# A hand-laid order for the attention, and modulation rows made in the layer that uses them

## The chip, the core and the metric

The kernel runs on one core of one Trainium2 chip. The metric is the time of one execution in microseconds of the device (us); lower is better. The engines meant below are PE (matrix multiplication), DVE (vector work on rows and columns), ACT (functions of one input, such as exp, and copies), POOL (a slower vector engine) and SP, which issues the transfers from the chip's memory. Each engine takes its instructions in the order in which they stand in its own queue; a semaphore makes one wait for another.

## The reference, cut to what matters

Two layers work on 1024 rows of 1024 numbers, in float32. A layer is a token mixer (convolution group, differential attention, gated chunk group, one output projection) and a channel mixer (up-projection to 2 x 2816, convolution of width 3, silu gate, down-projection). Each mixer is wrapped by a modulation from the conditioning vector `c`, and by a layer norm.

```python
c_act = jax.nn.silu(c)
for l in range(DEPTH):                                   # DEPTH = 2
    mod = (c_act @ w_ada[l] + b_ada[l])[:, None, :]
    sh1, sc1, g1, sh2, sc2, g2 = jnp.split(mod, 6, axis=-1)
    h = x * (1.0 + sc1) + sh1
    ...
    y = jnp.concatenate([y_a, y_b, y_c], axis=-1) @ w_out[l] + b_out[l]
    x = layer_norm(DEEPNORM_ALPHA * x + (1.0 + g1) * y, ln_g[l, 0], ln_b[l, 0])
    h = x * (1.0 + sc2) + sh2
    y = conv_ffn(h, w_up[l], b_up[l], conv_f_w[l], conv_f_b[l], w_down[l], b_down[l])
    x = layer_norm(DEEPNORM_ALPHA * x + (1.0 + g2) * y, ln_g[l, 1], ln_b[l, 1])
```

The six pieces of `mod` are numbered 0 to 5 in the kernel. 0, 1 and 2 (shift, scale, gate) belong to the token mixer, 3, 4 and 5 to the channel mixer.

The attention has 4 heads. A head has two softmax maps, each with its own queries and keys of 64 numbers; the values are 128 wide.

```python
for i in range(seq // ATTN_BLOCK):                       # 8 blocks of 128 queries
    s = jnp.einsum("bhmqd,bhmkd->bhmqk", qb, kb) * scale # m = 2 maps, keys 0 .. end
    p = jax.nn.softmax(jnp.where(mask, s, -jnp.inf), axis=-1)
    a = p[:, :, 0] - lam * p[:, :, 1]
    outs.append(jnp.einsum("bhqk,bhke->bhqe", a, vb))
o = rms_norm(o, subln_g) * (1.0 - lam_init)
```

## The kernel before

**Number format.** Every large product is split into a high and a low part and made of three matmuls (hi*hi, lo*hi, hi*lo; lines 130 to 132). A float32 operand is split by one ACT cast (line 125, tiles ending in `h`) and one subtraction on POOL or DVE (line 126, tiles ending in `l` or `L`).

**Stages of a layer.** First the modulated rows `h` are projected (`prj`, `ptm`), the convolution group and the chunk group are computed, and the queries, keys and values are written to memory. Then comes the attention with the first part of the output projection beside it. The rest of that projection (`og`), the residual and the layer norm follow (`boundary`: the rows are transposed back to columns, `tr`, line 333). Then the up-projection (`upb`), the down-projection (`og<-dn`) and a second `boundary`.

**The attention.** There are 32 units in a layer: 4 heads by 8 query blocks, in the order 7, 6, 3, 5, 2, 4, 1, 0 of the block number `i` (7, 6, 5, 4, 0, 1, 2, 3 in the last head). A unit has (i+1)*128 keys. One unit is: score matmuls on PE for both maps (line 733) and a mask (735); row maxima on DVE (754 or 756); exp with row sums on ACT (759); `rc`, `rho` and the difference of the two maps on DVE (762 to 767, here called diff); transposes on PE (774), copied by ACT (775); the product with the values on PE (778); scaling and sum of squares on ACT (780, 781). A unit with i of 4 or more is large: its two maps need two PSUM tiles of 1024 columns, and there are two; a small unit holds both maps in one tile. After a head come its norm (POOL line 138, DVE 789) and 8 transposes (801).

**The fill.** PE work that does not hang on the softmax is laid between: 16 chunks of the output projection over the convolution and chunk groups (4 row groups of `w_out`, 12 matmuls a chunk; here fillA) and 16 chunks over heads 0 and 1 (6 matmuls a chunk; here fill0). Each chunk ends in one PSUM bank, the only one of its kind, and DVE adds it to a row tile `r` (line 862, fill-add). Their weights are loaded, multiplied by the gate on POOL (`wout`, line 682), cast on ACT (`woh`) and subtracted on POOL (`wol`). In layer 0, POOL also adds a row to each of eight `r` tiles (line 871).

**What sets the order.** The code names units, heads and fills in program order, and a scheduler then lays each engine's queue by its own estimates and priorities. So a fill chunk can start before all of its weights are there, parts of several units interleave, and a late operand is passed by other work.

**The modulations.** Piece `idx` of layer `l` is one row of 1024: eight loads of 512 KB of `w_ada`, each multiplied and added on DVE (`macc` or `wada`, lines 258 and 260), then 8 one-column matmuls (`modp`, line 269) and small DVE work; a gate piece (2, 5) also has a transpose (`gatet`, line 286). A generator yields them in steps, one DVE operation over 1024 numbers in most. Before the change, layer 0's pieces 2 and 4 are made in its first stage, 3 in its attention, 5 at the start of its up-projection; all six of layer 1 (1, 0, 2, 3, 4, 5) follow in layer 0's up-projection (one step a tile of it) and what is left there (`later`) in layer 0's down-projection.

## Time and profile before

| what | us |
|---|---|
| median of 3 runs | 2440.98 (2439.22 to 2441.18) |
| the profiled execution | 2437.79 |
| its span | 2436.1 |
| first stage, layer 0 / layer 1, from `ptm` on | 205.0 / 190.1 |
| attention, layer 0 / layer 1 | 221.0 / 216.1 |
| up-projection, layer 0 / layer 1 | 426.2 / 422.8 |
| down-projection, layer 0 / layer 1 | 249.2 / 241.0 |
| from the last `og` of layer 0 to the first `prj` of layer 1 | 41.4 |

The stages are cut by PE's own rows: the attention runs from the first score matmul to the first `og` that follows (286.1 to 507.1 and 1492.1 to 1708.2 us of the span). PE is busy for 95% of the span, so a time is mostly read from what PE does and from the places where it stands still. A row of a timeline or of a group list has the line, the engine, the operation, what is written and read, and behind it the idle time of the engine just before, with what ended it.

### The profile page before, as it was taken

To read this page: it belongs to the slowest core of one execution; us is meant where nothing else is said; L and a number is where in the kernel's file an instruction comes from. 1 tells how busy PE (TensorE), PEld (TensorE's weight loads), DVE (VectorE), ACT (ScalarE), POOL (GpSimd) and SP (SyncE) were. 2 spreads that over 40 slices of the span, in tenths; PEclk is the share of its full clock that TensorE was granted. 3 is DMA by queue.
4 is the path that set the end of the run, shared out by engine and by line. 5 is a ranking of instruction groups with operands and counts; after the bars stand their busy time and mean duration, and the time that the engine had idled before them with its cause. 6 is when DMAs were issued, how large, how long until landed. Compare 5 with 4: busy or idle time off the path is not lost.

```text
span 2436.1 us, 28260 instructions
## 1 busy us (share of the span) xinstructions
PE 2308.1 (95%) x10846; PEld 1886.4 (77%) x10846; DVE 1956.1 (80%) x2650; ACT 1049.9 (43%) x1692; POOL 328.9 (13%) x165
## 2 busy tenths in 40 slices
PE   8998999979999999999959999999899999999996
PEld 7787778767888887788848877777688888878885
DVE  7898876778887888877978988657987777797857
ACT  4214754646554555311130257555654555561111
POOL 1143260410000000000020541214100000000003
PEclk9998999999999999999979999999999999999998
DMA  7433462122332333745523244320232222254301
GB/s 294 156 116 120 140 224 104 61 95 90 110 113 88 112 113 121 263 141 179 190 70 117 78 143 160 130 95 27 99 100 87 78 78 87 87 176 169 122 26 69
DMA packets 87672, 294.06 MB, mean 121 GB/s; under 512 B 9265, under 2 KB 18801, under 8 KB 86001
## 3 DMA queue, kind: packets, MB, share of 16 engines
q1 hardware_dynamic: 87536, 292.26, 35.4%
q8 instruction: 85, 1.39, 0.2%
q14 instruction: 51, 0.41, 0.1%
HBM read 228.23 MB, written 64.00 MB: 120 GB/s over the span
## 4 chain that ended last, share of the span: by engine, by line
PE 67%; DVE 17%; issue 6%; ACT 4%; DMA 3%; POOL 2%; SPq 0%; POOLq 0%; DVEq 0%; ACTq 0%
PE upb L1083 6%; PE upb L1084 6%; PE upb L1085 6%; PE og L130 5%; PE og L131 5%; PE og L132 5%; PE sc L733 3%; PE upd L1084 3%; PE upd L1085 3%; PE upd L1083 3%; DVE convacc L410 2%; PE pv L778 2%; PE of L130 2%; PE of L132 2%; PE of L131 2%
## 5 line engine op out<-in xcount | busy, mean ns | idle before, releaser
L1083 PE MATMUL upb<-comb,uw 128*128 128x512 f32 x704 | 274.9, 391 | 9.9 <-DVE upc L1107 5.0
L130 PE MATMUL og<-dn,dn 128*128 128x512 f32 x704 | 275.3, 391 | 2.6 <-ACT r L885 2.1
L131 PE MATMUL og<-dn,dn 128*128 128x512 f32 x704 | 274.5, 390 | 0.0
L132 PE MATMUL og<-dn,dn 128*128 128x512 f32 x704 | 274.3, 390 | 0.0
L1084 PE MATMUL upb<-comb,uw 128*128 128x512 f32 x704 | 274.0, 389 | 0.0
L1085 PE MATMUL upb<-comb,uw 128*128 128x512 f32 x704 | 273.9, 389 | 0.0
L1107 DVE TENSOR_TENSOR uw<-wu,uw 128x512 fp32r<-128x512 f32 x210 | 144.1, 686 | 125.3 <-ACT uw L1110 125.3
L1120 DVE SCALAR_TENSOR_TENSOR cv<-upc,pc,cv 128x1023 f32<-128x1023 f32 (+1 forms) x176 | 225.4, 1280 | 2.9
L138 POOL TENSOR_TENSOR lnrs<-lnrs,mhalf 128x1 f32<-128x1 f32 x32 | 24.8, 779 | 1421.4 <-DVE lnrs L137 1414.9
L887 DVE TENSOR_TENSOR r<-og,r 128x1024 f32<-128x1024 f32 x128 | 155.7, 1218 | 59.0 <-PE og L132 58.4
L410 DVE SCALAR_TENSOR_TENSOR convacc<-convy,pc,convacc 128x1023 f32<-128x1023 f32 (+14 forms) x120 | 176.2, 1469 | 2.3
L125 ACT CAST dn<-actr 128x1024 fp32r<-128x1024 f32 x44 | 46.1, 1049 | 298.1 <-issue 224.4
L1083 PEld LDWEIGHTS upb<-comb,uw 128*128 128x128 f32 x704 | 132.1, 188 | 41.0 <-DVE upc L1107 6.7
L1110 ACT CAST uw<-wu 128x512 fp32r<-128x512 f32 x210 | 121.7, 616 | 83.6 <-DVE wu L1107 77.1
L130 PEld LDWEIGHTS og<-dn,dn 128*128 128x128 f32 x704 | 132.2, 188 | 31.5 <-ACT r L885 3.4
L1085 PEld LDWEIGHTS upb<-comb,uw 128*128 128x128 f32 x704 | 132.2, 188 | 27.5
L132 PEld LDWEIGHTS og<-dn,dn 128*128 128x128 f32 x704 | 132.2, 188 | 27.4
L1084 PEld LDWEIGHTS upb<-comb,uw 128*128 128x128 f32 x704 | 132.2, 188 | 27.2
L131 PEld LDWEIGHTS og<-dn,dn 128*128 128x128 f32 x704 | 132.2, 188 | 26.8
L1083 PE MATMUL upd<-comb,uw 128*128 128x512 f32 x352 | 137.3, 390 | 0.0
L1085 PE MATMUL upd<-comb,uw 128*128 128x512 f32 x352 | 136.9, 389 | 0.0
L1084 PE MATMUL upd<-comb,uw 128*128 128x512 f32 x352 | 136.9, 389 | 0.0
(312 smaller groups left out, 5474.4 us busy)
## 6 DMA issues: line engine op xcount, KB each, us to landing
wada<-in_w_ada SPq DMA_DIRECT2D x96, 512.0 KB, 4.6
wu<-in_w_up_t SPq DMA_DIRECT2D x84, 512.0 KB, 3.6
d_act<-cv SPq DMA_DIRECT2D x44, 512.0 KB, 2.6
actr<-d_act SPq DMA_DIRECT2D x44, 512.0 KB, 4.6
wdn<-in_w_down SPq DMA_DIRECT2D x44, 512.0 KB, 4.2
win<-in_w_fm SPq DMA_DIRECT2D x24, 512.0 KB, 4.0
wtm<-in_w_tm SPq DMA_DIRECT2D x16, 512.0 KB, 3.7
wout<-in_w_out SPq DMA_DIRECT2D x16, 512.0 KB, 6.2
```

Of the source, the lines that this page charges most:

```text
L130: mm(ps, lh, rh, start=first, stop=False)
L131: mm(ps, lh, rl, start=False, stop=False)
L132: mm(ps, ll, rh, start=False, stop=last)
L410: nc.vector.scalar_tensor_tensor(out=acc[:, d:], in0=y[:, :S - d], scalar=w(30 - d), in1=acc[:, d:], op0=ALU.mult, op1=ALU.add)
L733: nc.tensor.matmul(ps[m][:, c0:c1], q[ms, isl], k[ms, c0:c1], start=n == 0, stop=n == 2 and c1 != w)
L887: nc.vector.tensor_tensor(out=r[t], in0=ps, in1=r[t], op=ALU.add)
L1083: mm(ps, w[:, 0, ks], hi[k], start=k == 0 and not more, stop=False, skip_group_check=True)
L1084: mm(ps, w[:, 0, ks], lo[k], start=False, stop=False, skip_group_check=True)
L1085: mm(ps, w[:, 1, ks], hi[k], start=False, stop=k == 3, skip_group_check=True)
L1107: v.tensor_tensor(out=o, in0=x, in1=y, op=op)
L1110: act.copy(self.up_w[n][:, 0], src)
L1120: v.scalar_tensor_tensor(out=u[:, d:], in0=c[:, :S - d], scalar=self.ffw[:, 2 - d, m:m + 1], in1=u[:, d:], op0=ALU.mult, op1=ALU.add)
```

## The change

The attention is taken out of the scheduler's hands on PE, ACT and DVE: inside `manual_schedule` these three run in program order, and the program is one loop over the 32 units `g`. POOL and SP are still ordered by the scheduler. The keys of head 3 are projected inside the loop (units 0 to 3) and not beside it. fillA starts at unit 8 and is done at unit 19; fill0 starts at unit 24, two chunks a unit. A unit's diff, transposes and value product are issued one unit later, and one modulation step ends each unit from 8 on. Each layer now makes its own pieces 3 and 4 in its attention and its own 5 in its up-projection; what remains for layer 0 to do ahead of layer 1 is 1, 0 and 2.

```diff
@@ first stage
-            self.bg.append(self.mix(self.mods(0, (2, 4)), self.conv_taps(l, self.y[0], self.acc[0], 0)))
+            self.bg.append(self.mix(self.mods(0, (2,)), self.conv_taps(l, self.y[0], self.acc[0], 0)))
...
+        with self.tc.manual_schedule(engines={nc.tensor.engine, nc.scalar.engine, nc.vector.engine}):
+            r = self.attention(l, H, self.X, O, stk, vp, grow, wk)
...
+    def attention(self, l, H, X, O, stk, vp, grow, wk):
+        order = (4, 5, 0, 1, 2, 3, 6, 7)
+        keys = self.key_chunks(l, 3, H, wk)
+        fillA = self.fill_chunks(self.lhsA, self.wA, r, order, 1.0 if l else ALPHA)
+        fill0 = self.fill_chunks(self.lhs0, self.wB, r, order)
...
+        for g, (h, n, i) in enumerate(units):
...
+            self.att_score(u, stk)
+            if prev:
+                self.att_diff(l, prev)
+            self.att_max(u)
+            if prev:
+                self.att_turn(prev, (O if g < 6 else X) + "c")
+            self.att_exp(u)
+            fills = keys if g < 6 else fillA if g < 20 else fill0
+            if not 6 <= g < 8 and not 20 <= g < 24:
+                next(fills, None)
+            if prev:
+                self.att_out(prev)
+            if g in (8, 10, 12, 14) or g >= 24:
+                next(fills, None)
+            if h and n == 1:
+                self.head_norm(*heads[h - 1], (0, 1))
+            if h and n == 2:
+                self.head_scale(*heads[h - 1], (0, 1))
+                self.head_turn(l, h - 1, O, heads[h - 1][0], (0, 1))
...
+            if g == 4:
...
+                raws = self.page(X + "a", "wout", shape=(P, 4, 1024))
+                for k in range(len(self.woA), 4):
+                    self.woA.append(self.scaled_wout(l, KA[k], grow, raws[:, k - 2]))
+            if 4 <= g < 8:
+                self.wA.append(self.split_wout(O, self.woA[g - 4]))
+            if h == 0:
+                t = order[n]
+                r[t] = self.load_res(t, ab) if n >= 5 else None
+                if n == 5:
+                    for t in order[:5]:
+                        r[t] = self.load_res(t, ab)
+            if h == 1 and n == 0:
...
+                late = self.mods(l, (3, 4))
...
+            if g in (20, 21):
+                self.lhs0.append(self.load_yb(l, g - 20, O))
+            if 20 <= g < 24:
+                self.wB.append(self.load_wout(l, g - 18, O, grow, self.page(O + "a", "wout")))
+            next(late, None)
+            prev = u
...
+    def out_fill_steps(self, lhs, w, r, t, scale):
...
+        for n in range(2):
+            pb = self.bank("of", "fill")
+            for k in range(len(lhs)):
+                self.mm3(pb, lhs[k][0][:, ts_], lhs[k][1][:, ts_], w[k][0][:, ns], w[k][1][:, ns], k == 0,
+                         k == len(lhs) - 1)
+            nc.vector.scalar_tensor_tensor(out=r[t][:, ns], in0=r[t][:, ns], scalar=scale, in1=pb, op0=ALU.mult,
+                                           op1=ALU.add)
+            yield
@@ up-projection
-        if l == 0:
-            later = self.mods(1, (1, 0, 2, 3, 4, 5))
-            mods = chain(self.mods(0, (5,)), later)
+        later = self.mods(l + 1, (1, 0, 2)) if l + 1 < L else iter(())
+        mods = chain(self.mods(l, (5,)), later)
```

The order moves at three places that matter below. On PE, the first large unit of layer 0: before, six matmuls of the first map (`sc_2189`) stood together and other work followed; the second map (`sc_2190`) came 32 rows on.

```order
L733 MATMUL sc_2189<-stk_1910,stk_1906 128x512
L733 MATMUL sc_2189<-stk_1910,stk_1908 128x512
L733 MATMUL sc_2189<-stk_1912,stk_1906 128x512
L735 LDWEIGHTS identb
L735 MATMUL sc_2189<-maskb,identb 128x128
L130 MATMUL prf_2248<-h_132,wh_2244 128x512
L131 MATMUL prf_2248<-h_134,wh_2244 128x512
```

Now the two maps alternate, matmul by matmul, in every unit.

```order
L734 MATMUL sc_2160<-stk_1877,stk_1871 128x512
L734 MATMUL sc_2161<-stk_1877,stk_1871 128x512
L736 LDWEIGHTS identb
L736 MATMUL sc_2160<-maskb,identb 128x128
L736 LDWEIGHTS identb
L736 MATMUL sc_2161<-maskb,identb 128x128
```

On POOL at the start of layer 0's attention, `wout` being the multiplied weights, `wol` their low parts, `yal` the low parts of the convolution group and `r` the row tiles, the queue before read:

```order
L126 TENSOR_TENSOR wol_2321<-wout_1666,woh_2320 128x1024
L126 TENSOR_TENSOR wol_2325<-wout_1798,woh_2324 128x1024
L126 TENSOR_TENSOR yal_2111<-ya_2024,yah_2110 128x1024
L682 TENSOR_TENSOR wout_2315<-wout_2315,grow_1664 128x1024 x2
L126 TENSOR_TENSOR wol_2329<-wout_2315,woh_2328 128x1024
L871 TENSOR_TENSOR r_2389<-r_2389,ab_2336 128x1024
L871 TENSOR_TENSOR r_2478<-r_2478,ab_2336 128x1024
L871 TENSOR_TENSOR r_2519<-r_2519,ab_2336 128x1024
L126 TENSOR_TENSOR wol_2333<-wout_2315,woh_2332 128x1024
```

Now it reads:

```order
L683 TENSOR_TENSOR wout_2428<-wout_2428,grow_1629 128x1024 x2
L988 TENSOR_TENSOR r_2487<-r_2487,ab_2426 128x1024
L988 TENSOR_TENSOR r_2490<-r_2490,ab_2426 128x1024
L988 TENSOR_TENSOR r_2496<-r_2496,ab_2426 128x1024
L126 TENSOR_TENSOR wol_2434<-wout_1631,woh_2433 128x1024
L126 TENSOR_TENSOR wol_2484<-wout_1763,woh_2483 128x1024
L988 TENSOR_TENSOR r_2493<-r_2493,ab_2426 128x1024
L126 TENSOR_TENSOR yal_2076<-ya_1989,yah_2075 128x1024
L126 TENSOR_TENSOR wol_2544<-wout_2428,woh_2543 128x1024
L988 TENSOR_TENSOR r_2499<-r_2499,ab_2426 128x1024
L988 TENSOR_TENSOR r_2502<-r_2502,ab_2426 128x1024
L126 TENSOR_TENSOR wol_2587<-wout_2428,woh_2586 128x1024
```

The two multiplications stand first, and all four `wol` behind them; six additions to `r` instead of three stand ahead of the last `wol`. In layer 1 there are no such additions.

On PE at the end of layer 0's down-projection, the last modulation of layer 1 stood between the last `og` and the transposes `tr`:

```order
L131 MATMUL og_9141<-dn_7400,dn_7397 128x512
L132 MATMUL og_9141<-dn_7399,dn_7398 128x512
L269 MATMUL modp_8625<-ones,macc_7560 128x1 x8
L286 MATMUL gatet_8638<-ident,gatec_8421 16x128
L333 MATMUL tr_8982<-ident,r_7441 128x128
```

Now `gatet` stands some 385 rows ahead of the last `og`, and the first half of the transposes stands among the last `og` matmuls:

```order
L333 MATMUL tr_8885<-ident,r_7435 128x128
L333 MATMUL tr_8894<-ident,r_7435 128x128
L130 MATMUL og_8957<-dn_7405,dn_7387 128x512
L131 MATMUL og_8957<-dn_7406,dn_7387 128x512
L132 MATMUL og_8957<-dn_7405,dn_7388 128x512
```

More of the change, by code (lines that the diff above doesn't have):

```diff
@@ L735, in score, with att_max @@
             nc.tensor.matmul(ps[m][:, i * P:w], self.identb, self.maskb, start=False, stop=True)
-    def attn_unit(self, l, at, stk, vp, i, ot, ss):
+    def att_max(self, u):
         nc = self.nc
-        w = (i + 1) * P
-        small = i < 4
-        sums = self.sm("sums", [P, 2], bufs=4)
-        mx = self.sm("mx", [P, 2], bufs=4)
-        if small:
-            ps2 = self.mm("sc")
+        w, ps = u["w"], u["ps"]
+        mx = u["mx"] = self.sm("mx", [P, 2], bufs=4)
+        if u["small"]:
+            nc.vector.tensor_reduce(out=mx, in_=u["ps2"].rearrange("p (m k) -> p m k", m=2)[:, :, :w], axis=AX.X,
+                                    op=ALU.max, negate=True)
+        else:
+            for m in range(2):
+                nc.vector.tensor_reduce(out=mx[:, m:m + 1], in_=ps[m][:, :w], axis=AX.X, op=ALU.max, negate=True)
@@ L745, in attn_unit, with att_score, att_exp @@
+    def att_score(self, u, stk):
+        u["w"] = (u["i"] + 1) * P
+        u["small"] = u["i"] < 4
+        if u["small"]:
+            ps2 = u["ps2"] = self.mm("sc")
+            u["ps"] = [ps2[:, 0:512], ps2[:, 512:1024]]
+        else:
+            u["ps"] = [self.mm("sc"), self.mm("sc")]
+        self.score(u["ps"], stk, u["i"])
+    def att_exp(self, u):
+        nc = self.nc
+        w = u["w"]
+        if u["small"]:
             p2 = self.page("tmp", "p")
-            ps = [ps2[:, 0:512], ps2[:, 512:1024]]
@@ L747, in attn_unit @@
-            pr = [p2[:, 0:512], p2[:, 512:1024]]
-        else:
-            ps = [self.mm("sc"), self.mm("sc")]
-            pr = [self.page("tmp", "p") for _ in range(2)]
-        self.score(ps, stk, i)
+            pr = u["p"] = [p2[:, 0:512], p2[:, 512:1024]]
+        else:
+            pr = u["p"] = [self.page("tmp", "p") for _ in range(2)]
+        sums = u["sums"] = self.sm("sums", [P, 2], bufs=4)
         for m in range(2):
-            if not small:
-                nc.vector.tensor_reduce(out=mx[:, m:m + 1], in_=ps[m][:, :w], axis=AX.X, op=ALU.max, negate=True)
@@ L1093, in up_phase @@
         s1, s2 = s[:, 0:512], s[:, 512:1024]
-        wa = [self.page("Ra", "wada") for _ in range(2 if l == 0 else 0)]
+        wa = [self.page("Ra", "wada") for _ in range(2)]
         cg, cv = self.page("Ra", "upc"), self.page("Ra", "upc")
@@ L1280, in ffn @@
                 if l + 1 < L:
-                    for ww in range(2):
-                        self.affine_cols(l + 1, ww)
+                    self.affine_cols(l + 1, 0)
                     pre = self.za_first(l + 1, A)
```

204 lines of the change are left out of this document (109 added, 95 removed).

## The prediction

> **What bounds the kernel now.** I read the page first (busy times, chain), then a table by stage, then single rows where PE stands still.
>
> ```profile
> PE 2308.1 (95%) x10846; PEld 1886.4 (77%) x10846; DVE 1956.1 (80%) x2650; ACT 1049.9 (43%) x1692; POOL 328.9 (13%) x165
> PE 67%; DVE 17%; issue 6%; ACT 4%; DMA 3%; POOL 2%; SPq 0%; POOLq 0%; DVEq 0%; ACTq 0%
> ```
>
> PE is the bound nearly everywhere; DVE is second, and holds 17% of the chain. The table by stage says where each of them matters (columns: window, its length, busy us of PE, PEld, DVE, ACT, POOL, then the granted clock).
>
> ```profile
> 81.00:286.00 205.00, 197.71 (x877) 162.50 (x877) 189.74 (x248) 71.14 (x79) 70.00 (x30) 0.95 0.38 126
> 286.10:507.10 221.00, 206.42 (x1170) 162.84 (x1170) 156.61 (x221) 124.97 (x317) 75.32 (x31) 0.95 0.33 115
> 552.20:978.40 426.20, 421.55 (x1870) 347.88 (x1869) 359.55 (x503) 221.68 (x320) 0.00 (x0) 1.00 0.34 110
> 978.40:1227.60 249.20, 247.83 (x1125) 205.34 (x1123) 206.68 (x210) 48.73 (x51) 1.93 (x2) 1.00 0.57 188
> 1227.60:1269.00 41.40, 15.70 (x80) 10.99 (x79) 35.04 (x50) 18.89 (x31) 13.96 (x10) 0.64 0.17 52
> 1302.00:1492.10 190.10, 185.93 (x848) 153.44 (x846) 171.57 (x229) 67.52 (x74) 66.75 (x27) 0.99 0.34 111
> 1492.10:1708.20 216.10, 202.79 (x1153) 158.74 (x1153) 141.83 (x210) 124.86 (x318) 54.20 (x23) 0.97 0.27 98
> 1752.70:2175.50 422.80, 417.53 (x1838) 344.44 (x1837) 340.62 (x479) 220.97 (x321) 0.00 (x0) 1.00 0.27 91
> 2175.50:2416.50 241.00, 239.74 (x1057) 197.71 (x1055) 177.37 (x176) 51.83 (x53) 12.83 (x9) 1.00 0.31 104
> ```
>
> Two things are to be seen. In the attention PE idles only 14.6 us (221.0 less 206.4) and 13.3 us, so a new order can gain there only by making PE's work shorter or by those few us. And the 41.4 us between the layers hold 15.7 us of PE: this is the worst place of the program. PE's timeline there:
>
> ```profile
> 1227.44 1.84 PE L269 MATMUL modp<-ones,macc 128*128 128x1 f32 x16
> 1251.32 0.38 PE L286 MATMUL gatet<-ident,gatec 128*16 128x128 f32 x1 [22.04 <-DVE gatec L283]
> ```
>
> PE waits 22 us for a small DVE operation of layer 1's gate. DVE was solid just before it (59.97 of 60.00 us):
>
> ```profile
> 1193.00:1253.00 60.00, 37.25 (x172) 30.57 (x171) 59.97 (x78) 5.55 (x6) 14.80 (x11) 0.83 0.33 106
> ```
>
> So the backlog of DVE sets the end of layer 0, and the modulation steps are part of it.
>
> **The change, part by part.** The sum is made against the profiled execution, 2437.8 us (a span of 2436.1 and 1.7 around it); the median of the runs, 2441.0, stands 3.2 above it.
>
> *Modulations moved out of layer 0's down-projection.* The steps of line 260 in that stage:
>
> ```profile
> 978.40:1227.60 249.20, 44.81 (x35) 1.00 0.57 188
> ```
>
> 35 steps of 1.28 us ran there. Three of layer 1's six pieces leave it (their 24 loads of 512 KB and some 24 steps, 31 us of DVE), and the last `gatet` stands far ahead of the end. The 22.0 us wait goes. What is late next is the layer norm of the last row tiles, an addition, statistics, POOL's power and a scaling of 1 to 2 us each, about 6 us, behind the last `og`; against that, half of the 16 groups of transposes now stands among the `og`, and these groups ran every 1.1 us (16 from 1251 to 1269), so 9 us leave the gap. -22 + 6 - 9 = **-25**. Bounds: -31 (nothing is late next) and -12 (DVE still 10 us behind). Inside the down-projection layer 0 took 8.2 us more than layer 1, which has no steps; with less than half of the steps left I take half, **-4** (0 to -8).
>
> *Piece 4 leaves layer 0's first stage,* where DVE is busy for 189.7 of 205.0 us. Layer 1 does the same stage without any step in 190.1. Half of the 14.9 us between them is **-7** (0 to -15).
>
> *Piece 5 is added to layer 1's up-projection.* Layer 0 pays 3.4 us (426.2 less 422.8) with 19 steps; ten steps are **+2** (0 to +4). PE covers the rest: 417.5 of 422.8 us.
>
> These four give -34.
>
> *Score matmuls in pairs, both layers.* The same six or twelve matmuls cost PE differently by their order:
>
> ```profile
> 1599.22 1.66 PE L733 MATMUL sc<-stk,stq 64*128 64x512 f32 x6
> 1608.12 2.07 PE L733 MATMUL sc<-stk,stq 64*128 64x512 f32 x12
> 1613.70 0.97 PE L733 MATMUL sc<-stk,stq 64*128 64x512 f32 x6
> 1632.06 0.79 PE L733 MATMUL sc<-stk,stq 64*128 64x384 f32 x6
> 334.71 0.62 PE L733 MATMUL sc<-stk,stk 64*128 64x256 f32 x6
> 335.47 0.55 PE L733 MATMUL sc<-stk,stk 64*128 64x128 f32 x6
> 335.26 0.28 PE L735 MATMUL sc<-maskb,identb 128*128 128x128 bf16 x2
> 1492.10:1708.20 216.10, 68.73 (x352) 40.14 (x288) 45.43 (x48) 51.20 (x128) 0.97 0.27 98
> ```
>
> Six of one map take 1.66 us, twelve that alternate between the maps 2.07 (they use 64 of PE's rows each and run side by side). The last row is all work on score tiles in layer 1: 68.7 us of PE, masks with them. With everything in pairs a head costs 2.07 for 1024 keys, 0.97 and another 0.79, 0.62 or 0.55 for the other large units (6.9 for the four), 0.97, 0.79, 0.62 and 0.55 for the small ones (2.9), and eight pairs of masks of 0.28: 12.0 us, 48 a layer. That is **-20.7 a layer**. [...]
>
> *New waits in the attention.* PE, ACT and DVE no longer pass a late operand. Without the pairs' gain PE's work is 206.4 and 202.8 us a layer; the waits are counted afresh on 185.7 and 182.1, so the old idle (-14.6, -13.3) goes into the sum too.
>
> First, fillA's start. The weights of its last two groups are loaded once a page of `h` is free, and POOL works them off in order:
>
> ```profile
> 319.69 6.51 POOL L682 TENSOR_TENSOR wout<-wout,grow 128x1024 f32<-128x1024 f32 x2
> 326.15 2.81 POOL L126 TENSOR_TENSOR wol<-wout,woh 128x1024 fp32r<-128x1024 f32 x1
> 328.92 8.62 POOL L871 TENSOR_TENSOR r<-r,ab 128x1024 f32<-128x1024 f32 x3
> 337.50 2.38 POOL L126 TENSOR_TENSOR wol<-wout,woh 128x1024 fp32r<-128x1024 f32 x1
> 1525.15 3.23 POOL L682 TENSOR_TENSOR wout<-wout,grow 128x1024 f32<-128x1024 f32 x1 [19.38 <-DMA wout<-in_w_out]
> L778 PE MATMUL pv<-vp,at 128*128 128x128 f32 x288 | 40.3, 283 | 0.0
> L774 PE MATMUL at<-ident,p 128*128 128x128 f32 x144 | 22.1, 275 | 0.2 <-DVE p L767 0.2
> ```
>
> In layer 0 the data came 33.6 us after the first score (319.7 less 286.1), in layer 1 33.0; the page is freed by the same projection of head 3, so I keep that. The new queue in layer 0 is then 6.5 + three additions 8.6 + two `wol` 5.2 + one addition 2.9 + `yal` 2.5 + `wol` 2.8 + two additions 5.7 + `wol` 2.4 = 36.6 us: ready 70 us after the first score. PE gets to unit 8 after the keys (48 matmuls of 0.227, 11 us), head 0 (12.0 of scores, and a quarter of 40.3 and 22.1 for value products and transposes, whose busy times overlap a little: 26), unit 8's score (2) and some 6 us of chain waits in units 4 to 7, which have no fill: 45. Some matmuls of the chunk can go ahead: **+20** in layer 0. Low end +9: `wol` ready where it was (339.9 less 286.1 = 54). In layer 1, without additions, 33 + 20 = 53: **+5** (0 to 8). The waits in units 4 to 7 themselves are **+6** (3 to 10).
>
> Second, from fillA to fill0. The eight pages of fillA's operands are free only after its last chunk. The chain that follows (load, cast, subtract, four multiplications) is in the trace:
>
> ```profile
> 434.40 0.32 SPq L811 DMA_DIRECT2D ybr<-d_yb  x1
> 456.84 5.56 POOL L126 TENSOR_TENSOR wol<-wout,woh 128x1024 fp32r<-128x1024 f32 x2
> ```
>
> Some 26 us to the second `wol`. PE then has units 20 to 23 (about 9 us) and one large score (2): 26 less 11 is **+15** a layer (8 to 22). Before, the scheduler put scores of head 3 there.
>
> Third, DVE in order. In units with two chunks (8, 10, 12, 14) the second fill-add and a modulation step stand ahead of the diff that PE's next transposes need.
>
> ```profile
> L862 DVE SCALAR_TENSOR_TENSOR r<-r,of 128x512 f32<-128x512 f32 x31 | 21.2, 684 | 21.9 <-PE of L132 21.5
> L767 DVE SCALAR_TENSOR_TENSOR p<-p,rho,p 128x1024 f32<-128x1024 f32 x4 | 6.0, 1509 | 0.1
> L754 DVE TENSOR_REDUCE mx<-sc 128x1 f32<-128x1024 f32 x8 | 9.8, 1219 | 6.0 <-PE sc L735 6.0
> L759 ACT ACTIVATE p<-sc,mx 128x1024 f32<-128x1024 f32 x8 | 8.9, 1118 | 7.3 <-DVE mx L754 7.3
> ```
>
> 0.68 + 1.28 + 0.4 (`rc`, `rho`) + 1.5 = 3.9 us behind the second chunk, of which the next score covers 2: four times 2 is **+8** (4 to 12). In head 3 a large unit's chain from its score (2) over a maximum (1.2), two exps (1.3 each with their sums) to diff (1.9) is 7.7 us, about what PE has (transposes 0.9, two half chunks 2.8, values 1.8, next score 2); I take 1.3 us a unit, **+10** (4 to 16).
>
> Fourth, the tail behind the last unit's exp, by rows of like size: diff 0.8, transposes and copy 1.1, values 1, scaling and squares 0.9, norm on DVE and POOL 1.4, scaling 0.7, transposes 0.5, of which little is covered now: **+6** (3 to 8).
>
> Layer 0: -20.7 - 14.6 + 20 + 6 + 15 + 8 + 10 + 6 = +30. Layer 1: -20.7 - 13.3 + 5 + 6 + 15 + 8 + 10 + 6 = +16. The extra modulation steps are in the third wait, their loads lie beside a DMA busy for a third. Together +46, less 34: **+12**, 2450 us on the profiled execution, **2453** as a median.
>
> **The rivals.** *The waits swallow each other* (faster, 0.40). A PE that is late once gives POOL and DVE time to catch up, so the terms cannot all be paid. With the low ends (9, 3, 8, 4, 4, 3 in layer 0; 0 for the first in layer 1) the layers give -4 and -12; with -34 the time is 2391. Halfway to my sum it is 2422. My waits come to 115 us in all, and what speaks for faster to 103 (34, twice 20.7, 14.6 and 13.3): the change is slower only if more than 90% of them are paid. For it: the 22 us between the layers and the pairs are the firmest numbers here. Against: the waits for weights and pages (the 19.38 us of POOL above) end by a load or a queue that nothing in the new order hastens, and DVE and PE are close in load.
>
> *A colder clock* (slower, 0.15). In this attention two short stalls brought the clock down:
>
> ```profile
> 295.56 1.77 PE L733 MATMUL sc<-stk,stk 64*128 64x512 f32 x6 [2.17 <-ACT rot L380]
> 299.15 2.60 PE L733 MATMUL sc<-stk,stk 64*128 64x512 f32 x6 [1.60 <-ACT p L759]
> 296.00:306.00 10.00, 7.88 (x22) 5.46 (x21) 8.75 (x9) 9.61 (x14) 2.35 (x1) 0.55 0.15 54
> ```
>
> Ten us at 0.55 cost 4.5. With 60 us of waits a layer in many places, three such stretches a layer more are +27: 2480. The mean clock of the attention is 0.95 and 0.97 now; the case is decided by whether it falls below 0.9. [...]
>
> *The pairs do not run side by side* where the maps lie in two PSUM tiles (0.03): +41, 2494. The row of twelve at 1608.12 speaks against it.
>
> **How the numbers follow.** My sum and what lies near it on the slow side 0.34, the cold clock 0.15, no pairs 0.03, waits swallowed 0.40; 0.08 is left within 0.2% (5 us), about what a measurement of this kernel tells from no change. Slower is 0.52. The range reaches to half of the low ends' gain and to the cold clock with a little more: 2405 to 2500; the likeliest case alone has 2446 to 2480.
>
> **What would show it.** The row of `gatet` without its 22 us, and some 15 us from the last `og` to the first `prj`: the first term. Work on score tiles near 48 us of PE a layer: the pairs. PE waiting for POOL `wol` at the first chunk in layer 0 but hardly in layer 1, for 10 us or more between fillA and fill0, and for DVE's diff in each unit with two chunks: the waits. If attention's windows come out under 221 and 216 us, my waits are wrong and the kernel is faster; if DVE is solid to the end of layer 0 again, the gain between the layers is wrong.

## The result and the profile after

The changed kernel takes 2549.98 us (median of 4 runs, 2536.92 to 2553.36); the kernel before took 2440.1 beside it (4 runs, 2437.57 to 2441.18). The ratio is 1.0442, with a 95% interval of 1.0404 to 1.048: slower by 4.4%. The prediction was 2453, so it is 97 us too low. The profiled execution took 2553.36 us with a span of 2551.3, 115.2 above the span before.

First the page's busy times of the changed kernel, and its chain of waits.

```profile
PE 2310.9 (91%) x10846; PEld 1891.7 (74%) x10846; DVE 1949.2 (76%) x2650; ACT 1057.7 (41%) x1692; POOL 334.1 (13%) x165
PE 63%; DVE 18%; issue 6%; ACT 4%; POOL 4%; DMA 4%; SPq 0%; POOLq 0%; DVEq 0%; ACTq 0%
```

PE is busy for the same time as before (2308.1), over a longer span. That alone is a riddle: the pairs should have made PE's work shorter by some 40 us. The table by stage resolves it; here are its rows of the two attentions and of the gap between the layers (stage, its length, busy us of PE, PEld, DVE, ACT, POOL, granted clock, DMA's share, GB/s).

```profile
273.90:566.40 292.50, 211.13 (x1185) 167.76 (x1185) 162.11 (x230) 129.00 (x317) 76.77 (x31) 0.85 0.29 101
1290.40:1307.70 17.30, 10.08 (x50) 7.54 (x48) 16.38 (x18) 15.80 (x26) 11.64 (x5) 0.64 0.40 122
1530.40:1815.70 285.30, 207.67 (x1185) 166.04 (x1185) 161.50 (x229) 129.06 (x317) 54.75 (x23) 0.85 0.29 102
```

| stage | before | after | difference |
|---|---|---|---|
| first stage, layer 0 / layer 1 | 205.0 / 190.1 | 194.9 / 189.4 | -10.1 / -0.7 |
| attention, layer 0 / layer 1 | 221.0 / 216.1 | 292.5 / 285.3 | **+71.5 / +69.2** |
| up-projection, layer 0 / layer 1 | 426.2 / 422.8 | 429.2 / 427.6 | +3.0 / +4.8 |
| down-projection, layer 0 / layer 1 | 249.2 / 241.0 | 247.6 / 239.2 | -1.6 / -1.8 |
| last `og` of layer 0 to first `prj` | 41.4 | 17.3 | **-24.1** |
| all the rest (start, layer 1's first projections, two boundaries, end) | 223.3 | 228.3 | +5.0 |

The gap between the layers has closed. The two attentions took 141 us more. In each, PE now idles for 81.4 and 77.6 us (before 14.6 and 13.3), and its clock is 0.85 (before 0.95 and 0.97). The work on score tiles alone, same columns, layer 1:

```profile
1530.40:1815.70 285.30, 50.17 (x352) 29.09 (x288) 44.47 (x49) 50.09 (x128) 0.85 0.29 102
```

So the pairs do bring 18.5 us (68.7 before). The 32 one-column matmuls (`modp`) of pieces 3 and 4, new in this attention, add 3.7. PE's 202.8 us should so have become 188.0, but are 207.7: about 20 us are lost because PE works more slowly. Layer 1 adds up: 18.5 us less score work, 3.7 of `modp`, 19.7 of slower PE, 64.3 more idle, together +69.2.

What PE waits for in layer 1's attention (waiting instruction, what released it; us in total, times, longest):

```profile
PE at L792 <- DVE p L781: 31.4, 20, 5.3
PE pv L800 <- ACT at L793: 19.9, 9, 7.2
PE obt L829 <- DVE ot L814: 11.2, 5, 5.4
PE sc L734 <- ACT rot L380: 8.8, 1, 8.8
PE sc L734 <- DMA stk<-d_k: 2.9, 1, 2.9
```

The same five lines cost 30.6, 19.3, 11.2, 8.7 and 2.8 in layer 0, with one more, and that is the only wait for fillA's weights:

```profile
PE of L131 <- POOL wol L126: 5.7, 1, 5.7
```

PE's timeline shows where they are (start, us, instruction; in brackets the idle time just before it):

```profile
1539.65 2.92 PE L734 MATMUL sc<-stk,stk 64*128 64x512 f32 x11 [8.76 <-ACT rot L380]
1588.45 1.33 PE L792 MATMUL at<-ident,p 128*128 128x128 f32 x5 [5.25 <-DVE p L781]
1626.42 1.94 PE L829 MATMUL obt<-ident,ot 128*128 128x128 f32 x8 [2.01 <-DVE ot L814]
1637.15 0.87 PE L792 MATMUL at<-ident,p 128*128 128x128 f32 x6 [1.58 <-DVE p L781]
1714.57 1.65 PE L800 MATMUL pv<-vp,at 128*128 128x128 f32 x6 [7.25 <-ACT at L793]
1725.30 2.51 PE L800 MATMUL pv<-vp,at 128*128 128x128 f32 x10 [6.50 <-ACT at L793]
1814.97 1.11 PE L829 MATMUL obt<-ident,ot 128*128 128x128 f32 x4 [5.37 <-DVE ot L814]
```

By place, layer 1's waits are 8.8 us at the first unit (the second map's tile is still held by a projection until ACT has read it), 13.6 in units 1 to 7 (12.6 of them from unit 4 on), 16.1 beside fillA, 17.4 between fillA and fill0, 11.7 in head 3, and 9.7 in the tail: 77.3.

The two causes behind most rows are orders, not loads. DVE, around the 1.58 us wait:

```profile
1633.77 0.69 DVE L978 SCALAR_TENSOR_TENSOR r<-r,of 128x512 f32<-128x512 f32 x1 [1.44 <-PE of L132]
1634.38 1.28 DVE L260 SCALAR_TENSOR_TENSOR wada<-wada,cact 128x1024 f32<-128x1024 f32 x1
...
1636.07 1.02 DVE L781 SCALAR_TENSOR_TENSOR p<-p,rho,p 128x768 f32<-128x768 f32 x1
```

The fill-add stands still for 1.44 us until the chunk's last matmul; the modulation step runs behind it, and only then the diff that PE's next transposes need. ACT, around the 7.25 us wait:

```profile
1713.09 1.04 ACT L125 CAST woh<-wout 128x1024 fp32r<-128x1024 f32 x1 [5.73 <-POOL wout L683]
1714.04 0.47 ACT L793 COPY at<-at 128x384 f32<-128x384 f32 x1
```

Here a cast of fill0's weights waits for POOL, and the copy that PE needs queues behind it, though fill0 itself is units away.

### The profile page after: what moved, and what is told of

Read it like the earlier page. It is cut to its first block, busy times and chain, and to the rows that moved or that the text cites. A ratio compares the mean times of both kernels' runs of the same rounds, so it can differ in the third digit from the quotient of the medians.

```text
span 2551.3 us, 28246 instructions
## 1 busy us (share of the span) xinstructions
PE 2310.9 (91%) x10846; PEld 1891.7 (74%) x10846; DVE 1949.2 (76%) x2650; ACT 1057.7 (41%) x1692; POOL 334.1 (13%) x165
## 4 chain that ended last, share of the span: by engine, by line
PE 63%; DVE 18%; issue 6%; ACT 4%; POOL 4%; DMA 4%; SPq 0%; POOLq 0%; DVEq 0%; ACTq 0%
PE upb L1176 6%; PE upb L1177 6%; PE upb L1178 6%; PE og L130 5%; PE og L131 5%; PE og L132 5%; PE upd L1177 3%; PE upd L1176 3%; PE upd L1178 3%; PE of L130 2%; PE of L131 2%; PE of L132 2%; DVE convacc L410 2%; DVE p L781 2%; PE at L792 2%
## 5 line engine op out<-in xcount | busy, mean ns | idle before, releaser
L978 DVE SCALAR_TENSOR_TENSOR r<-r,of 128x512 f32<-128x512 f32 x64 | 44.0, 687 | 141.8 <-PE of L132 134.7
L1176 PE MATMUL upd<-comb,uw 128*128 128x512 f32 x352 | 137.3, 390 | 0.0
L1177 PE MATMUL upd<-comb,uw 128*128 128x512 f32 x352 | 137.0, 389 | 0.0
```

The costliest lines, as they stand in the source:

```text
L1176: mm(ps, w[:, 0, ks], hi[k], start=k == 0 and not more, stop=False, skip_group_check=True)
L1177: mm(ps, w[:, 0, ks], lo[k], start=False, stop=False, skip_group_check=True)
```

## The experiments

All ratios are against the kernel before on the same chip, which stayed near 2440 us. "Waits" are PE's, in the attention.

### The two parts without the hand-laid order

`e_mods` is the kernel before with the modulations placed as in the change, and nothing else.

```diff
-            ...self.mods(0, (2, 4))...
+            ...self.mods(0, (2,))...
...
-                        late = self.mods(0, (3,))
+                        late = self.mods(l, (3, 4))          # both layers
...
-            later = self.mods(1, (1, 0, 2, 3, 4, 5))
-            mods = chain(self.mods(0, (5,)), later)
+        later = self.mods(l + 1, (1, 0, 2)) if l + 1 < L else iter(())
+        mods = chain(self.mods(l, (5,)), later)
```

> The kernel before with the modulations moved as in the change (2 alone in layer 0's first stage, 3 and 4 in each layer's own attention, 5 in its own up-projection, 1, 0, 2 ahead of layer 1); the attention's order stays with the scheduler. Theory: the moved modulations are the good half of the change; from the stages of the changed kernel (first stage -10, between the layers -25, down-projections -3, up-projections +8) and some 5 us more for ten more steps in layer 1's attention, 2440 - 25 = 2415 (2405 to 2425). Rival: the steps in both attentions are what makes the change slow; then the attentions are longer than 221 and 216 us by 20 or more each and the time is 2440 or above.

Measured: 2446.59, ratio 1.0025 (1.0013 to 1.0037). The gap closed by 24.7 us and layer 0's first stage by 10.1, as in the change, but the attentions grew by 19.2 and 17.1. The expectation failed and its rival held: the placement is no gain by itself. In the window of layer 1's attention:

```profile
1475.30:1708.50 233.20, 214.59 (x1185) 168.12 (x1185) 165.96 (x232) 127.38 (x318) 56.57 (x23) 0.92 0.35 125
```

Of the 17 us only 5.3 are idle (18.6 against 13.3). PE's busy time is 11.8 longer: 3.7 are the 32 one-column matmuls (1185 against 1153), and the other 8 are work that is the same, at a clock of 0.92 instead of 0.97.

`e_pairs` is the kernel before with PE alone held in program order inside one unit's score, so that the two maps alternate.

```diff
-        self.score(ps, stk, i)
+        with self.tc.manual_schedule(engines={nc.tensor.engine}):
+            self.score(ps, stk, i)
```

> The kernel before, with the matmuls of one unit's scores alone held in program order on PE, so that the two maps alternate in large units too; all else with the scheduler. Theory: work on score tiles falls from 68 to about 50 us a layer and the attentions by most of it: 2440 - 30 = 2410 (2400 to 2425). Rival: the pairs need both PSUM tiles free at once, so PE waits for the second tile what it gains, and the time stays within 10 us of before; or a wait at the first unit of a layer, 8.7 us in the changed kernel, comes in here too.

Measured: 2437.47, ratio 0.9988 (0.9977 to 0.9999): 3 us less, as the rival had it. Layer 1's attention, and in it the score tiles alone:

```profile
1491.80:1709.20 217.40, 194.03 (x1153) 150.85 (x1153) 142.48 (x210) 124.89 (x318) 53.47 (x23) 0.93 0.27 97
1491.80:1709.20 217.40, 49.83 (x352) 27.34 (x288) 44.23 (x48) 50.76 (x128) 0.93 0.27 97
```

The scores are 18.9 us shorter, as reckoned, yet the stage is 1.3 longer. PE's busy time fell only by 8.8 (clock 0.93 instead of 0.97), and its idle time rose from 13.3 to 23.4. I read it so: PE has got ahead of the softmax chain, it waits, and with the waits the clock falls.

`e_mods_pairs` joins both edits.

> Both of the first two together on the kernel before. If they add, 2440 - 25 - 30 = 2385 (2370 to 2400). If pairs only move a wait, it equals the run with the modulations alone.

Measured: 2440.0, ratio 0.9998 (0.9989 to 1.0007). Together they give 7 us over `e_mods`, not the 30 expected.

### Which engine's order costs what

These are the changed kernel with the scheduler given back some or all of the three engines. `e_free`:

```diff
-        with self.tc.manual_schedule(engines={nc.tensor.engine, nc.scalar.engine, nc.vector.engine}):
+        with nullcontext():
```

> The changed kernel with its new loop, but the attention left to the scheduler on PE, ACT and DVE. Theory (strict order is the loss): the waits of 80 us a layer and the lowered clock go, attentions of 215 to 235 us, time 2400 to 2440. Rival (the loop itself is the loss: diff a unit later, fill0 from unit 24 on only, w_out's later groups loaded at units 20 to 23): the attentions stay above 260 us and the time above 2490.

`e_pe` keeps only PE, `e_pe_act` PE and ACT, `e_pe_dve` PE and DVE in program order:

```diff
+        with self.tc.manual_schedule(engines={nc.tensor.engine}):                          # e_pe
+        with self.tc.manual_schedule(engines={nc.tensor.engine, nc.scalar.engine}):        # e_pe_act
+        with self.tc.manual_schedule(engines={nc.tensor.engine, nc.vector.engine}):        # e_pe_dve
```

> The changed kernel with PE alone in program order in the attention, ACT and DVE with the scheduler. By the three runs before it (DVE free 2500, ACT free 2539, all free 2462): if PE's own order costs little, 2465 to 2475; if it is what remains between 2500 and 2462, 2485 to 2500.

> The changed kernel with PE and ACT in program order, DVE left to the scheduler. Theory: DVE's order makes most of the 31 us of waits for the diff and part of the 11 us before a head's transposes; 2550 becomes 2490 to 2525. If DVE's order is not at fault: above 2540. With both this and the run without ACT near 2550, it is PE's own order that sets the time.

> The changed kernel with PE and DVE in program order in the attention, ACT left to the scheduler. Theory: ACT's order makes the waits of PE's value products for the copies (19 to 20 us a layer, two of 7 us in units 21 and 22, where a cast of a late operand stands in front) and what follows; they go, and 2550 becomes 2500 to 2525. Rival: the late operands bind anyway: above 2540.

| kernel | in program order | us | ratio (95%) | attention, layer 0 / 1 |
|---|---|---|---|---|
| `e_free` | none | 2462.18 | 1.0087 (1.0071 to 1.0104) | 248.6 / 241.3 |
| `e_pe` | PE | 2474.68 | 1.0143 (1.0127 to 1.0159) | 250.5 / 250.9 |
| `e_pe_act` | PE, ACT | 2500.35 | 1.0241 (1.0224 to 1.0258) | 264.9 / 257.3 |
| `e_pe_dve` | PE, DVE | 2539.44 | 1.0403 (1.0386 to 1.042) | 281.9 / 278.5 |
| the change | PE, ACT, DVE | 2549.98 | 1.0442 (1.0404 to 1.048) | 292.5 / 285.3 |

DVE's fixed order is the dear one: giving DVE back is worth 50 us (2550 to 2500), giving ACT back 11. For `e_pe_dve` I had expected 2500 to 2525; it missed by 14, because the waits pass from ACT to DVE. The waits for the diff and for ACT's copy, layer 1, first of `e_pe_act`, then of `e_pe_dve`:

```profile
PE at L792 <- DVE p L781: 14.5, 6, 4.8
PE pv L800 <- ACT at L793: 17.2, 9, 6.3
```

```profile
PE at L792 <- DVE p L781: 37.1, 22, 5.3
PE pv L800 <- ACT at L793: 7.7, 9, 1.9
```

With ACT free the long waits for copies are gone (7.2 to 1.9 at most), and the diff is waited for 5.7 us longer. And `e_free`, with no engine held, has not got the kernel before's time either (2462 lies between what the theory and the rival of its expectation gave); the score tiles in its layer 1 attention:

```profile
1486.40:1727.70 241.30, 73.22 (x352) 43.09 (x288) 45.95 (x52) 50.86 (x128) 0.89 0.35 120
```

It is 16 us above `e_mods`: the new loop, from whose program order the scheduler takes its priorities, is itself worse, and the scheduler parts the pairs again (73.2 us). `e_pe` has the pairs (50.8) and pays with waits for them. Taken one after the other, the modulations (2447), the loop (2462), PE's order (2475), ACT's (2500) and DVE's (2550) cost 6, 16, 12, 26 and 50 us, which are the 110; with DVE's order ahead of ACT's these two cost 65 and 11.

`e_early` is the change with the modulation step issued right behind the unit's row maxima and ahead of its fill-adds, where DVE has a pause while PE works on the chunk.

```diff
             self.att_max(u)
+            next(late, None)
...
-            next(late, None)
             prev = u
```

> The changed kernel with one move: a unit's modulation step is issued behind its row maxima and not at its end, so that it runs beside the fill's matmuls and stands no more between the last fill-add and the diff of the unit. Theory (DVE in order): PE's waits for the diff, 31 us a layer, fall by up to 1.28 us for each of the 18 steps; 12 to 18 us less a layer, and some 5 by the clock: 2505 to 2530. Rival: the maxima or fill-adds become late in their place, or the steps are not what delays the diff: 2540 or above.

Measured: 2517.56, ratio 1.0316 (1.03 to 1.0331), as expected. The wait for the diff in layer 1 falls by a third, and the attentions by 17.8 and 15.1 us:

```profile
PE at L792 <- DVE p L781: 20.8, 15, 5.3
```

So 32 us of the 110 hang on where one DVE operation of 1.28 us stands in a unit.

### What the cold clock costs

`e_warm` puts useless matmuls into PE's waits, 198 a layer, written into the tile that PE is about to overwrite anyway. They were of 512 columns:

```diff
+    def warm(self, pb, vp, n):
+        for _ in range(n):
+            self.nc.tensor.matmul(pb[:, 0:512], vp[:, 0, :], vp[:, 0:4, :]..., start=True, stop=True)
...
             pb = self.bank("at")
+            if b0 == 0:
+                self.warm(pb, u["vp"], n)          # n by unit, after the waits measured there
```

> The changed kernel with matmuls of no use put in front of PE's waits: 198 a layer, each 512 columns wide, into the PSUM tile that the waiting instruction writes next (some 0.23 us each, 45 us a layer), sized a little below the waits measured in the changed kernel. They add work and take no wait away. Theory (lowered clock): the mean clock of the attentions rises from 0.85 to 0.95 or more, PE's other rows get shorter by some 20 us a layer, and the time falls from 2550 to 2505 to 2530. Rival (the clock follows, but costs nothing, since other engines set the pace; or there is no such link): the time is 2545 to 2590.

Measured: 2736.67, ratio 1.1214 (1.1196 to 1.1233). The dummies were far longer than the waits (attentions 386.1 and 376.9), so this run can't decide on the gain. It does show the cause of the cold: with PE kept busy the clock of both attentions is 0.97 and 0.98, with all else in the same order.

`e_warm2` is the same with 128 columns, reckoned at 0.22 us each, 44 us a layer.

```diff
-            ...matmul(pb[:, 0:512], vp[:, 0, :], vp[:, 0:4, :]..., start=True, stop=True)
+            ...matmul(pb[:, 0:P], vp[:, 0, :], vp[:, 1, :], start=True, stop=True)
```

> As the first run with useless matmuls, whose rows turned out to cost some 0.85 us each (169 us a layer) and not 0.23; here each is 128 columns wide, by the rows of the value products 0.22 us, 44 us a layer, in the same places and of the same number. Theory (lowered clock): the clock of the attentions rises from 0.85 towards 0.95, the other rows lose some 20 us a layer, and the added work lies mostly in waits: 2510 to 2545. Rival (no cost by the clock): 2555 to 2600, the added work where it is longer than a wait.

Measured: 2527.17, ratio 1.035 (1.0332 to 1.0368): 23 us **faster** than the change, with some 100 us more work on PE. Layer 1's attention in `e_warm2`, the rows of its dummies (line 786), and the value products, in `e_warm2` and then in the change (count, busy us, mean ns, idle before):

```profile
1519.10:1790.80 271.70, 240.02 (x1582) 200.80 (x1581) 156.62 (x223) 126.09 (x313) 54.43 (x23) 0.94 0.31 107
L786 PE MATMUL at<-vp 128*128 128x128 f32 x198 | 25.5, 279 | 0.0
L786 PE MATMUL pv<-vp 128*128 128x128 f32 x116 | 15.1, 294 | 1.9 <-ACT pv L810 1.9
L786 PE MATMUL obt<-vp 128*128 128x128 f32 x82 | 9.8, 275 | 0.0
L807 PE MATMUL pv<-vp,at 128*128 128x128 f32 x288 | 40.3, 288 | 4.7 <-ACT at L799 4.7
```

```profile
L800 PE MATMUL pv<-vp,at 128*128 128x128 f32 x288 | 44.5, 307 | 19.9 <-ACT at L793 19.9
```

The dummies are busy for 50.4 us, more than the 44 expected. The idle time and the dummies together are 31.7 + 50.4 = 82.1 us, 4.5 more than the 77.6 us of waits in the change: the dummies took waiting time and little else. The real work went from 207.7 to 240.0 - 50.4 = 189.6 us, 18 less, and 18 less 4.5 are the stage's 13.6. The clock's part of the loss is so shown, not only argued, and most of it can be had back without mending one wait.

### Why the moved modulations cost 17 to 19 us an attention

`e_mod5` is the kernel before with layer 1's piece 5 alone moved to its own up-projection, so that nothing is added to the attention; `e_mod5_pairs` adds the pairs.

```diff
-            later = self.mods(1, (1, 0, 2, 3, 4, 5))
-            mods = chain(self.mods(0, (5,)), later)
+            later = self.mods(1, (1, 0, 2, 3, 4))
+            mods = chain(mods, later)                  # mods = self.mods(l, (5,)) in both layers
```

> The kernel before with one move: layer 1's piece 5 (the gate that PE waited 22 us for at the end of layer 0) is made in layer 1's own up-projection; all other pieces stay, none comes into an attention. Theory: the gap between the layers falls from 42 us to about 18 (or to 30, if the nine steps that stay more than in the changed kernel keep DVE solid), the up-projection of layer 1 pays 5, the attentions stay at 221 and 216: 2440 - 15 = 2425 (2415 to 2435). Rival: DVE's backlog at the end of layer 0 is made by the residual and stays, and the gap with it: 2440 or above.

> The same with the score matmuls of a unit held in program order on PE. If pairs bring 3 us as they did on the kernel before: 3 less than the run without them, about 2422.

Measured: 2437.33, ratio 0.999 (0.998 to 0.9999), and 2424.98, 0.9937 (0.9925 to 0.995). The gap fell by 22.5 us, but layer 0's down-projection took 9.9 more, layer 1's up-projection 5.5 and its attention 5.6 (clock 0.95): the backlog that is no longer paid at the end is partly paid elsewhere, and the run is 12 us above the 2425 expected. The pairs brought 12 us here and 3 in `e_pairs`; I had expected 3. Why the same shorter scores are worth more here I can't say.

Four kernels take `e_mods` apart. `e_mods_none` leaves the steps and loads of pieces 3 and 4 out in both layers. `e_mods_short` keeps their number and loads (with one more a piece) but lets each DVE step work on 32 of 1024 columns. `e_mods_xc` puts their tiles into two small pages, taken from the four of the transposed maps, instead of the page that head 3's keys need next. `e_mods_fast` issues two steps behind each unit, so that the pieces are done after nine units.

```diff
-                        late = self.mods(l, (3, 4))
+                        late = iter(())                                       # e_mods_none
...
+            c = slice(0, 32 if idx in (3, 4) else 1024)                       # e_mods_short
...
-                        mt = self.page(H + "a", "wada", shape=(P, 4, 1024))   # e_mods_xc
-                        self.mod_tile = [mt[:, i] for i in range(4)]
+                        self.mod_tile = [self.page(H + "c", "wada"), self.page(H + "c", "macc")]
...
                         next(late, None)
+                        next(late, None)                                      # e_mods_fast
```

> The run with the moved modulations alone, without any step of pieces 3 and 4 (left out: they are set to their bias, and their 32 loads, 32 long DVE operations and their matmuls are gone). It tells what those steps cost in the attentions at all. Theory (the steps, by their time, loads and page together): attentions of 216 to 222 us, time 2400 to 2412. Rival (the attention's length hangs on something else that moved with them, as the shorter first stage): they stay near 233 to 240.

> The run with the moved modulations alone, where pieces 3 and 4 work on 32 of their 1024 columns (the rest of the row is left out: the results of these pieces are wrong; one load of 512 KB a piece is added to fill the row's tile). Each of the 16 long steps in an attention costs DVE some 0.1 us in place of 1.28; the loads, the page that they hold and the places of the steps stay. Theory 1 (DVE's time, 18 x 1.28 = 23 us a layer, lengthens the attentions from 221 and 216 to 240 and 233): they fall back to 215 to 225 and the time to 2405 to 2415. Theory 2 (the page: it takes one of two pages for the heads' keys, so that heads 2 and 3 load their keys only after the head ahead is done): they stay at 230 or more, 2435 to 2447.

> The run with the moved modulations alone, with the attention's row and load tile in two of the four pages of the transposed maps and not in a page of the keys. DVE's work is the same. Theory 2 (the page of the keys): the keys of heads 2 and 3 load 40 to 50 us earlier in layer 1, the attentions fall to 218 to 226, and the time to 2410 to 2422. Theory 1 (DVE's time): they stay at 233 to 240 and the time within 5 us of 2447.

> The run with the moved modulations alone, two steps behind each unit in place of one, so that the 18 are done after 9 units (8 to 16) and not after 18. In the runs so far the attentions keep pace until 150 us after their first score and lose their 17 us behind it, in head 3. Theory (the steps and their page hurt only there, where heads 2 and 3 lack keys and fill): attentions 218 to 226, time 2408 to 2422. Rival (each step costs its share wherever it stands): 233 to 240, 2440 to 2450.

| kernel | us | ratio (95%) | attention, layer 0 / 1 | layer 1: PE idle, clock |
|---|---|---|---|---|
| `e_mods` | 2446.59 | 1.0025 (1.0013 to 1.0037) | 240.2 / 233.2 | 18.6, 0.92 |
| `e_mods_short` | 2442.09 | 1.0008 (0.9998 to 1.0019) | 238.5 / 232.6 | 17.4, 0.92 |
| `e_mods_xc` | 2446.3 | 1.0029 (1.0016 to 1.0042) | 235.3 / 236.4 | 16.3, 0.90 |
| `e_mods_fast` | 2423.26 | 0.9932 (0.9919 to 0.9944) | 226.9 / 225.1 | 14.7, 0.95 |
| `e_mods_none` | 2413.31 | 0.9893 (0.9878 to 0.9908) | 225.5 / 215.0 | 13.0, 0.98 |

Without the steps layer 1's attention is what it was (215.0, clock 0.98). So the steps are the cause there. Layer 0's stays 4.5 us longer than before, although even piece 3's steps, which it had before, are gone; that part has another cause, which I don't know. Neither their DVE time (`short`: 4 us) nor their page (`xc`: nothing) is it alone. The five kernels differ less in PE's idle time (13.0 to 18.6 us) than in PE's busy time (202.0 to 220.1), and the longest have the lowest clock. In `e_mods` the clock stood at half for a stretch in which PE was never idle:

```profile
1649.40:1659.60 10.20, 10.20 (x31) 0.50 0.00 0
```

Their timing counts: done early they cost 23 us less. In `e_mods` head 3's first keys are loaded late, since their page is held (SP's issue in the kernel before, in `e_mods`, in `e_mods_xc`; layer 1's attentions begin at 1492.1, 1475.3 and 1475.5):

```profile
1596.70 0.41 SPq L715 DMA_DIRECT2D stk<-d_k  x1
```

```profile
1630.31 0.43 SPq L715 DMA_DIRECT2D stk<-d_k  x1
```

```profile
1581.83 0.43 SPq L715 DMA_DIRECT2D stk<-d_k  x1
```

That is 105, 155 and 106 us into the attention, and 139 in `e_mods_fast`. So `e_mods_xc` has its keys as early as before and gains nothing by it; but it also leaves the transposed maps two pages less, and is no pure test. Which of DVE's time, the page, the loads and the 32 `modp` matmuls binds stays open: `short` and `xc` each took one away and gained next to nothing, and no run took the loads or the matmuls alone.

`e_mods_xc_pairs` and `e_mods_fast_pairs` add the pairs of `e_pairs`.

> The same with each unit's score matmuls in program order on PE. On the kernel before this brought 3 us, with piece 5 alone moved 12. If the page was the limit: 2400 to 2412, the fastest of all; if not: about 2440 as with the old page.

> The same with each unit's score matmuls in program order on PE: by the theory 3 to 12 us less than the run without them, 2398 to 2415, the fastest of all; by the rival about 2440.

Measured: 2436.34, ratio 0.9981 (0.9969 to 0.9993), and **2413.33, ratio 0.9886 (0.9872 to 0.9899)**. The second is as fast as `e_mods_none`, which lacks the steps and the pairs, and beats the kernel before by 27 us and the change by 137. Its two attentions:

```profile
274.80:500.20 225.40, 197.84 (x1186) 154.35 (x1185) 159.98 (x233) 125.56 (x316) 72.92 (x31) 0.94 0.38 131
1461.50:1680.70 219.20, 196.88 (x1186) 154.96 (x1185) 158.75 (x231) 125.65 (x317) 52.94 (x23) 0.93 0.39 132
```

They are still 4.4 and 3.1 us longer than before, at a colder clock (0.94 and 0.93, before 0.95 and 0.97); what it gains is the gap (24.8 us) and the first stage.

## Why the prediction was wrong, step by step

*The gap between the layers, -25:* right, -24.1. *Down-projection of layer 0, -4:* -1.6. *Piece 4 leaving the first stage, -7:* -10.1. *Piece 5 in layer 1's up-projection, +2:* +4.8, and layer 0's took 3.0 more without a step added. The four give -31.0 where I had -34.

*Score matmuls in pairs, -20.7 a layer:* the work shrank by 16.4 in layer 0 and 18.5 in layer 1, at a colder clock (0.85 in both). As a price on PE the step was right. As a gain it was not: alone, in `e_pairs`, it is worth 3 us in both layers together. The two attentions, +46 in the sum, came out at +141: of these 95 us, 44 are waits and 51 are PE's work.

*New waits in the attention, +65 and +50:* this is the first step that failed: 115 us in the sum, 159 measured (81.4 and 77.6 us of idle time). In layer 1:

| term | predicted | measured |
|---|---|---|
| first unit | none | 8.8 |
| units 4 to 7 (measured: 1 to 7) | 6 | 13.6 |
| fillA's start | 5 | 0 |
| DVE in order, beside fillA | 8 | 16.1 |
| fillA to fill0 | 15 | 17.4 |
| head 3 | 10 | 11.7 |
| tail | 6 | 9.7 |

The first unit I had not seen: the second map's tile was free early enough for a scheduler that put other work first, not for a fixed order. The term for DVE counted only units with two chunks; waits of 0.3 to 2.3 us for the diff came in nearly every unit, and the head norms (`obt`, 11.2 us in five waits) were not in any term but the tail. fillA to fill0 has nearly the right size (the chain that I took as 26 us runs 28.0 in the rows shown, from 434.40 to 462.40), but another form: I had fill0's first chunk wait for POOL; in fact ACT's copies queue behind the cast that waits for POOL, three units sooner. In layer 0, fillA's start cost 5.7 instead of 20. `wol` was ready at 74 us (I had 70), but PE itself came 23 us later than the 45 that I had reckoned, after its other waits: this much the waits do swallow each other, as the first rival said. It held for this one term only.

*The clock, at nothing in the sum:* the second step that failed. I held PE's work at 185.7 and 182.1 us, as if the clock stayed; it was 211.1 and 207.7, 51 us more. Of these, 5.5 are `modp` matmuls that no term held, 6.5 are what the pairs brought less, and 39 are slower work, 19 and 20 us a layer. I had put the cold clock into a rival of 0.15, with six stretches of 4.5 us, +27 together. Its own sign was met, a mean clock below 0.9 (0.85 in both layers), and its price was too small: three more stretches a layer, where 16 of the 28 slices of 10 us in layer 1 lie below 0.9. The error was to take it as an alternative to the sum. The waits that the sum counted bring it (filled with dummies, the clock is 0.97 and 0.98 in `e_warm`, 0.92 and 0.94 in `e_warm2`): when PE idles for a quarter of a stage (here 77.6 of 285.3 us), the clock has to be priced on what is left. The three stretches around the 2.01 us wait for the head norm (window, length, PE busy, granted clock):

```profile
1612.30:1622.60 10.30, 9.28 (x63) 1.00 0.17 52
1622.60:1632.80 10.20, 8.19 (x43) 0.83 0.32 102
1632.80:1643.00 10.20, 8.62 (x56) 1.00 0.30 104
```

One idle time of 2.01 us; from its end on the granted clock was 0.50 for 3.4 us (1626.43 to 1629.84), with 1.00 on both sides: by the clock, 1.7 us lost. The eight transposes behind the wait took 1.94 us. In layer 0 the same wait of 2.01 us (ended at 375.6) is followed by the same eight transposes in 1.06 us; there the clock of 0.50 came 1.5 us later (377.15 to 380.56), over other work. So the loss did not always stand right behind the wait. Nor did the length of a wait decide. The waits of 1.58, 1.71 and 1.84 us that follow in layer 1 cost nothing of the kind (clock 1.00 from 1636 to 1661), nor does one of 2.27 us, but a later one of 1.58 us does:

```profile
1664.90 0.41 PE L792 MATMUL at<-ident,p 128*128 128x128 f32 x2 [2.27 <-DVE p L781]
1663.50:1673.80 10.30, 8.40 (x46) 1.00 0.81 305
1673.80:1684.00 10.20, 9.89 (x63) 0.83 0.15 51
1701.41 1.49 PE L792 MATMUL at<-ident,p 128*128 128x128 f32 x6 [1.58 <-DVE p L781]
1694.20:1704.50 10.30, 8.47 (x52) 0.86 0.67 208
```

Its six transposes took 1.49 us, against 0.87 behind the 1.58 us wait at 1637. In the third row the clock fell with PE idle for only 0.3 us; 16 one-column matmuls, 1.84 us, had run just before. These two cold stretches are as long as the first, 3.4 us at 0.50 (1677.63 to 1681.04 and 1701.52 to 1704.93). No limit for one wait fits what is seen here: 0.3, 1.58 and 2.01 us were followed by a cold stretch, and 2.27 us passed. What starts a single one is not shown; the clock in this trace goes back and forth between 0.50 and 1.00.

*The moved modulations inside the attention, covered:* the third step that failed, and it was hidden by the sum. I put the extra steps "in the third wait" and their loads beside a DMA busy for a third. Under the scheduler, without any new order, they cost 19.2 and 17.1 us (`e_mods`), so that the placement as a whole, -34 in my sum, is +6 as a run.

Shown by runs are the cost of DVE's order (50 us, or 32 by the place of the step alone), of ACT's (11), of the steps in both attentions under the scheduler (33, `e_mods_none`, with those of piece 3 that layer 0 had before), and the clock's share by `e_warm2`. The first rival, the waits with their low ends, is refuted by the 159 us of waits; and taking some of them away, in `e_early` and `e_pe_act`, takes 32 and 50 us off, without coming under 2440. The third rival, that pairs don't run side by side, is refuted by 50.2 us of score work.

## What to carry to other kernels

A fixed order on several engines at once made every late operand a stall of PE, and the dear place was the helper engine's queue: look for what stands ahead of the operand that PE waits for (here a step of 1.28 us, worth 32 us by its place), before counting what the order saves on PE. Price the clock together with the waits: idle time scattered over a stage cost a further quarter of itself here (39 us beside 159). And a saving on the busiest engine was a gain only so far as its suppliers kept up: 18.9 us of shorter scores in layer 1 left its attention as long as it was in `e_pairs` (1.3 us more), and background work cost less when it was over early (`e_mods_fast`, 23 us).

## What was not expected of the hardware

Useless matmuls made a kernel faster: some 100 us of them, nearly all in waiting time, 23 us gained (2527 against 2550), with a clock of 0.92 and 0.94 instead of 0.85. A single idle time of 2.01 us was followed by 3.4 us at a clock of 0.50, one of 1.58 us by 3.4 us as well, and one of 2.27 us by none in the 12 us behind it. And in `e_mods` the clock of 0.50 lasted through 10.2 us in which PE was busy throughout; score matmuls of one map at a time stood there (three in 1.65 us from 1650.59 on), but no run shows whether that is the reason.

Some operations of DVE took far longer than their kind does elsewhere. A modulation step is 1.28 us (in `e_mods` at 1615.61); in the same run one took 3.39 while POOL was subtracting over 1024 columns, and the next one, from 1632.71, took 3.37 (rows of DVE's and POOL's timelines, by their start):

```profile
1626.21 2.61 POOL L126 TENSOR_TENSOR ybL<-ybr,ybh 128x1024 fp32r<-128x1024 f32 x1
1626.51 3.39 DVE L260 SCALAR_TENSOR_TENSOR wada<-wada,cact 128x1024 f32<-128x1024 f32 x1
1628.78 3.32 POOL L126 TENSOR_TENSOR wol<-wout,woh 128x1024 fp32r<-128x1024 f32 x1
```

The diff that stood between the two steps came late for PE, which waited 3.44 us for it, its longest wait in that attention. That POOL is the cause of the first slow step is only argued from the overlap; no row here shows POOL beside the second, and no run tried it by itself.
